# Three of four loads of an upsampling kernel issued from ScalarE's queue instead of SyncE's

## The chip, the cores and the metric

The kernel runs on one core of a Trainium2 chip. The metric is the device time in microseconds of one execution; the median of several runs is given. A profile of one execution shows what each engine and each DMA queue did, on a clock that starts with the core's first recorded instruction. Its length is called the span.

## The reference

Nearest-neighbour upsampling by 2 in both directions: every input value is written four times. The input is 16 x 64 x 64 x 64 in float32 (16.78 MB), the output 16 x 64 x 128 x 128 (67.11 MB).

```python
for i in range(new_h):
    for j in range(new_w):
        result[:, :, i, j] = x[:, :, i // scale_factor, j // scale_factor]
```

## The kernel before

The 65,536 image rows of 64 values are laid over 128 partitions, so each partition holds R = 512 rows, contiguous in DRAM. One SBUF tile, `mem`, holds everything: at its end the whole input (`xt`, 512 x 64 values for each partition), in front of that a free part of 79 rows' output size.

The input comes in four loads (line 195), all issued from SyncE: rows 0 to 8, 8 to 256, 256 to 480 and 480 to 512. They are called load 1 to load 4 here.

The output is made in nine steps (store 0 to store 8, with `rows = [52, 40, 52, 63, 52, 64, 63, 63, 63]` input rows for each partition). In each step VectorE expands 9/16 of the step's rows (line 215) and ScalarE the others (line 216) into a part of `mem`, and a DMA stores the result. Stores 2 to 6 are issued from GpSimd (line 218), the other four from SyncE (line 222). The steps' output places alternate between the start of `mem` and its end, where they overwrite input rows that have been read already; so a copy waits for the store that used its place before, and each engine waits for semaphores only. Nothing is planned by cost: the order on each queue is the order of the program.

The first store has one more wait, put in by hand: it is held until load 3 has landed ("stores begin as the loads end"). Both halves of step 0 need load 2, and VectorE's half needs load 1 too.

Two functions edit the built program at its end. `begin_before_barrier` takes SyncE's first four instructions, the loads, and puts them in front of SyncE's drain in the opening block, so that they are issued ahead of the barrier of all engines (line 249) that opens the kernel. `close_early` rearranges the closing barrier, so that only the last store is waited for at the end.

ScalarE has an activation table load behind the opening barrier, then its copies.

Of the kernel before, what the change touches and what calls it, by code (L numbers as in the profile page):

```python
# [6 lines left out]

EARLY = 4  # L10


def begin_before_barrier(nc):

    blocks = nc.main_func.blocks
    main, body = blocks[0], blocks[1]
    sp = mybir.EngineType.SP
    loads = [i for i in body.instructions if i.engine == sp][:EARLY]  # L20
    for load in loads:
        assert isinstance(load, mybir.InstDMACopy), type(load)
        assert not (load.sync_info and load.sync_info.on_wait)
    names = [i.name for i in loads]
    body.instructions = [i for i in body.instructions if i.name not in names]
    kept = list(main.instructions)
    at = next(
        n
        for n, i in enumerate(kept)
        if i.engine == sp and isinstance(i, mybir.InstDrain)  # L30
    )
    kept[at:at] = loads
    main.instructions = kept


def close_on_gpsimd(nc):
# [117 lines left out]
@with_exitstack  # L154
def kernel(
    ctx: ExitStack,
    tc: tile.TileContext,
    x: bass.AP,
    scale_factor: int,
    out: bass.AP,  # L160
):
    nc = tc.nc
    nc.at_finalize(begin_before_barrier)
    nc.at_finalize(close_early)
    P = nc.NUM_PARTITIONS
    s = int(scale_factor)
    B, C, H, W = x.shape
    R = B * C * H // P
    fdt = x.dtype

    xp = x.rearrange("b c h w -> (b c h) w").rearrange("(p r) w -> p r w", p=P)
    op = out.rearrange("b c (h hd) w -> (b c h) (hd w)", hd=s).rearrange(
        "(p r) w -> p r w", p=P
    )

    rows = [52, 40, 52, 63, 52, 64, 63, 63, 63]
    GROW = s * s
    FREE = 79
    WF = FREE * GROW * W
    assert sum(rows) == R
    mem_pool = ctx.enter_context(tc.tile_pool(name="mem", bufs=1))
    mem = mem_pool.tile([P, WF + R * W], fdt, name="mem")
    xt = mem[:, WF:].rearrange("p (r w) -> p r w", r=R)

    HEAD = 8
    cuts = [0, HEAD, R // 2, R - 32, R]
    loads = [
        nc.sync.dma_start(out=xt[:, lo:hi], in_=xp[:, lo:hi])  # L195
        for lo, hi in zip(cuts, cuts[1:])
    ]

    def expanded(r0, r1):
        return (  # L200
            xt[:, r0:r1].unsqueeze(2).unsqueeze(4).to_broadcast([P, r1 - r0, s, W, s])
        )

    r0 = 0
    before = (0, 0)
    for n, k in enumerate(rows):
        size = k * GROW * W
        at = 0 if n % 2 == 0 else WF + r0 * W - size
        assert at >= before[1] or at + size <= before[0]
        before = (at, at + size)  # L210
        u = mem[:, at : at + size].rearrange(
            "p (k a w b) -> p k a w b", k=k, a=s, w=W
        )
        kv = k * 9 // 16
        nc.vector.tensor_copy(out=u[:, :kv], in_=expanded(r0, r0 + kv))  # L215
        nc.scalar.copy(out=u[:, kv:], in_=expanded(r0 + kv, r0 + k))  # L216
        if 2 <= n < len(rows) - 2:
            store = nc.gpsimd.dma_start(  # L218
                out=op[:, r0 : r0 + k, :], in_=u, single_packet=True
            )  # L220
        else:
            store = nc.sync.dma_start(out=op[:, r0 : r0 + k, :], in_=u)  # L222
        if n == 0:
            tc.add_manual_dep(
                store.ins,
                loads[-2].ins.name,
                mybir.DependencyInfo(
                    mybir.DependencyClass.Sync, mybir.DependencyReason.DATA
                ),
                reason="stores begin as the loads end",  # L230
            )
        r0 += k
# [35 lines left out]
```

## Time and the profile before

| what | value |
|---|---|
| runs, median (lowest to highest) | 197.26 us (197.16 to 197.34) |
| profiled execution: span | 195.8 us |
| profiled execution: its own time | not listed apart from its span; the span is 1.5 us below the median of the runs |
| VectorE, ScalarE, GpSimd busy | 69.6, 51.4, 3.0 us |
| bytes moved, mean rate | 83.89 MB, 428 GB/s |
| load 2 issued from SyncE to landing | 21.3 us |
| load 3 issued from SyncE to landing | 37.8 us |

The profile calls the engines DVE (VectorE), ACT (ScalarE), POOL (GpSimd) and SP (SyncE); "SPq" and "ACTq" are the queues of instructions that are not counted as work, such as DMA issues, drains and waits. "L195" is line 195 of the kernel. In a row of tenths, each digit is the busy share of one of 40 equal slices. A chain lists, in order of time, start, length and what the time went to, followed back from the last instruction.

### The profile page before, as it was taken

To read this page: it belongs to the slowest core of one execution; us is meant where nothing else is said; L and a number is where in the kernel's file an instruction comes from. 1 tells how busy PE (TensorE), PEld (TensorE's weight loads), DVE (VectorE), ACT (ScalarE), POOL (GpSimd) and SP (SyncE) were. 2 spreads that over 40 slices of the span, in tenths; PEclk is the share of its full clock that TensorE was granted. 3 is DMA by queue.
4 is the path that set the end of the run, shared out by engine and by line. 5 is a ranking of instruction groups with operands and counts; after the bars stand their busy time and mean duration, and the time that the engine had idled before them with its cause. 6 is when DMAs were issued, how large, how long until landed. Compare 5 with 4: busy or idle time off the path is not lost.

```text
span 195.8 us, 108 instructions
## 1 busy us (share of the span) xinstructions
DVE 69.6 (36%) x9; ACT 51.4 (26%) x10; POOL 3.0 (2%) x9
## 2 busy tenths in 40 slices
DVE  0000596000039289069007205930692002960000
ACT  2000548000036083063920006666000003900000
POOL 0000000000000100100100100010000000000000
DMA  9999889699899989899999899999999999999994
GB/s 391 493 415 415 375 387 551 295 455 522 348 442 418 537 370 500 370 422 422 422 422 522 348 522 428 428 428 428 422 422 422 422 422 422 448 514 501 435 422 211
DMA packets 1872, 83.89 MB, mean 428 GB/s; under 512 B 208, under 2 KB 208, under 8 KB 336
## 3 DMA queue, kind: packets, MB, share of 16 engines
q1 hardware_dynamic: 1152, 45.35, 53.8%
q0 software_dynamic: 720, 38.54, 45.4%
HBM read 16.78 MB, written 67.11 MB: 428 GB/s over the span
## 4 chain that ended last, share of the span: by engine, by line
DMA 73%; DVE 15%; issue 1%; SPq 1%; DVEq 0%; POOLq 0%
DMA out_dram<-mem 54%; DMA mem<-in_x_dram 19%; DVE mem L215 15%; SPq L195 0%; SPq L222 0%; DVEq L215 0%; POOLq L218 0%; POOLq L263 0%
## 5 line engine op out<-in xcount | busy, mean ns | idle before, releaser
L215 DVE COPY mem<-mem 128x8960 f32<-128x8960 f32 (+3 forms) x9 | 69.6, 7739 | 104.9 <-DMA out_dram<-mem 83.1
L216 ACT COPY mem<-mem 128x7168 f32<-128x7168 f32 (+2 forms) x9 | 50.1, 5572 | 117.5 <-DMA out_dram<-mem 89.8
L218 POOL DMA_DIRECT2D out_dram<-mem x5 | 2.8, 560 | 126.8 <-DVE mem L215 111.2
L216 ACT ACT_TABLE_LOAD x1 | 1.3, 1283 | 2.2 <-PEq L249 2.2
L249 POOL MEMSET const-float32-0.0<- 128x1 f32 x1 | 0.1, 99 | 0.2 <-issue 0.2
L249 POOL MEMSET const-bfloat16-1.0<- 128x1 bf16 x1 | 0.1, 102 | 0.0
L249 POOL MEMSET const-float32-1.0<- 128x1 f32 x1 | 0.1, 99 | 0.0
L249 POOL MEMSET const-uint8-127<- 128x1 uint8 x1 | 0.1, 99 | 0.0
## 6 DMA issues: line engine op xcount, KB each, us to landing
out_dram<-mem POOLq DMA_DIRECT2D x2, 8064.0 KB, 29.9
out_dram<-mem SPq DMA_DIRECT2D x2, 8064.0 KB, 24.8
out_dram<-mem POOLq DMA_DIRECT2D x2, 6656.0 KB, 22.6
mem<-in_x_dram SPq DMA_DIRECT2D x1, 7936.0 KB, 21.3
mem<-in_x_dram SPq DMA_DIRECT2D x1, 7168.0 KB, 37.8
out_dram<-mem SPq DMA_DIRECT2D x1, 6656.0 KB, 18.1
out_dram<-mem SPq DMA_DIRECT2D x1, 5120.0 KB, 29.7
mem<-in_x_dram SPq DMA_DIRECT2D x1, 1024.0 KB, 39.8
```

The lines of the kernel that those rows point to most:

```text
L215: nc.vector.tensor_copy(out=u[:, :kv], in_=expanded(r0, r0 + kv))
L216: nc.scalar.copy(out=u[:, kv:], in_=expanded(r0 + kv, r0 + k))
L218: store = nc.gpsimd.dma_start(out=op[:, r0 : r0 + k, :], in_=u, single_packet=True)
L249: nc = _bacc.Bacc("TRN2", target_bir_lowering=False, num_devices=1)
```

## The change

Load 1 stays on SyncE's queue; loads 2, 3 and 4 are issued from ScalarE's. The function that moves loads ahead of the opening barrier now does so for both engines: one load in front of SyncE's drain, three in front of ScalarE's. Line numbers behind the edit grow by two. Nothing else differs: the copies, the stores, the hand-made wait and the places in `mem` are the same.

```diff
-EARLY = 4
+EARLY = {mybir.EngineType.SP: 1, mybir.EngineType.Activation: 3}
...
-    sp = mybir.EngineType.SP
-    loads = [i for i in body.instructions if i.engine == sp][:EARLY]
...
-    at = next(
-        n
-        for n, i in enumerate(kept)
-        if i.engine == sp and isinstance(i, mybir.InstDrain)
-    )
-    kept[at:at] = loads
-    main.instructions = kept
+    for engine, count in EARLY.items():
+        loads = [
+            i
+            for i in body.instructions
+            if i.engine == engine and isinstance(i, mybir.InstDMACopy)
+        ][:count]
...
+        at = next(
+            n
+            for n, i in enumerate(kept)
+            if i.engine == engine and isinstance(i, mybir.InstDrain)
+        )
+        kept[at:at] = loads
+        main.instructions = kept
...
     cuts = [0, HEAD, R // 2, R - 32, R]
+    queues = [nc.sync, nc.scalar, nc.scalar, nc.scalar]
     loads = [
-        nc.sync.dma_start(out=xt[:, lo:hi], in_=xp[:, lo:hi])
-        for lo, hi in zip(cuts, cuts[1:])
+        queue.dma_start(out=xt[:, lo:hi], in_=xp[:, lo:hi])
+        for queue, lo, hi in zip(queues, cuts, cuts[1:])
     ]
```

More of the change, by code (lines that the diff above doesn't have):

```diff
@@ L18, in begin_before_barrier @@
     main, body = blocks[0], blocks[1]
-    sp = mybir.EngineType.SP
-    loads = [i for i in body.instructions if i.engine == sp][:EARLY]
[L21 to L26, printed above, removed]
-    at = next(
-        n
-        for n, i in enumerate(kept)
-        if i.engine == sp and isinstance(i, mybir.InstDrain)
-    )
-    kept[at:at] = loads
-    main.instructions = kept
+    for engine, count in EARLY.items():
[4 more added lines that the diff above has]
+        ][:count]
+        assert len(loads) == count
+        assert not any(i.sync_info and i.sync_info.on_wait for i in loads)
+        names = [i.name for i in loads]
+        body.instructions = [i for i in body.instructions if i.name not in names]
+        kept = list(main.instructions)
+        at = next(
[5 more added lines that the diff above has]
+        main.instructions = kept
 def close_on_gpsimd(nc):
```

## The prediction

> **What bounds the kernel now.** I read the page first: busy time and queues, then the chain that ended last.
>
> ```profile
> span 195.8 us, 108 instructions
> ...
> DVE 69.6 (36%) x9; ACT 51.4 (26%) x10; POOL 3.0 (2%) x9
> ...
> DMA  9999889699899989899999899999999999999994
> ...
> q1 hardware_dynamic: 1152, 45.35, 53.8%
> q0 software_dynamic: 720, 38.54, 45.4%
> ...
> DMA 73%; DVE 15%; issue 1%; SPq 1%; DVEq 0%; POOLq 0%
> ```
>
> VectorE and ScalarE are idle two thirds of the time. The DMA queues' packets fill 53.8 + 45.4 = 99.2% of what 16 engines have in 195.8 us: the kernel is a transfer of 83.89 MB. The chain in order of time, merged, shows where it starts and where it is handed on:
>
> ```profile
> 0.00 0.37 SPq L195
> 0.37 0.05 issue
> 0.42 0.42 SPq L195
> 0.85 0.04 issue
> 0.89 37.79 DMA mem<-in_x_dram
> ...
> 38.77 0.35 SPq L222
> ...
> 39.29 29.69 DMA out_dram<-mem
> ...
> 79.15 40.20 DMA out_dram<-mem x2
> ...
> 129.52 35.38 DMA out_dram<-mem
> ```
>
> Rates by stage, from landings on this chain. The load of 1,024 KB and the first two stores (12,800 KB, 13.11 MB) land between 38.68 and 68.97: 433 GB/s. The next three stores (21.89 MB) land between there and 119.35: 434 GB/s. The last four (33.16 MB) run to 195.77: 434 GB/s. The first three loads, 15.73 MB, would take 36.2 us at 434, yet land at 38.68. So all slack is about 2.4 us at the very start, before the stream runs at full rate; later the engines never run dry. A change of queues can win only there, and can lose wherever it makes a gap.
>
> The start, from the packet records of the trace: load 1 (8 rows) is issued at 0.00, its first packet starts at 1.005 and the 16 engines finish it between 1.73 and 2.28. Load 2 (248 rows) is issued at 0.42. Its packets, 63,488 bytes each, take 2.342 us in the steady part; the engines begin their second one between 4.52 and 5.05, so the first counts as a full-rate packet started between 2.18 and 2.70. Between the end of load 1 and that point each engine loses 0.42 to 0.45 us on average: it has run out of load 1 and load 2 is not flowing yet. That is all this change can reach.
>
> **The change part by part.** *Load 2 moves to the front of another queue.* In SyncE's queue it stood behind one issue of 0.37 and a gap of 0.05, and began at 0.42. On ScalarE nothing stands in front of it. When ScalarE gets there is seen from the opening barrier, line 249 (minimum, median and maximum in ns, then first and last start in us), and what an issue costs from line 195:
>
> ```profile
> L249 ACTq DRAIN  x1: 8/8/8, 0.1 to 0.1; - x1
> ```
>
> ```profile
> L195 SPq DMA_DIRECT2D mem<-in_x_dram x4: 373/428/432, 0.0 to 1.4; - x4
> ```
>
> ScalarE's drain starts at 0.127 in the record, and the loads are put just ahead of it. So load 2 is issued at 0.13 instead of 0.42, 0.30 us earlier. No DMA is issued by ScalarE in the trace of before. I bound its cost by the nearest rows: 0.33 to 0.43 for SyncE's issues, 0.53 to 0.67 for GpSimd's. I take SyncE's 0.37 to 0.43, since these are the same transfers, byte for byte. At the upper end, 0.67, load 2's issue would end at 0.80, against 0.42 + 0.42 = 0.85 now, so even GpSimd's issue cost leaves 0.05. Below, a cheaper issue gains little more: load 2 cannot flow before load 1's packets are through, 0.42 to 0.45 earlier than now. The lead of 0.30 lies inside that cap, so I count it whole: **-0.30 us**, bounds 0 and -0.45.
>
> The Trainium skill speaks against hoping for more: "DMA: Bandwidth & Descriptors", section "Issuing engines are not separate DMA queues", says that DMAs from several engines run on the same 16 DMA engines and that issuing them concurrently saves only the sequencer's issue time. By that rule the sum would be at most one issue, -0.42 us and 196.84. The stages at 433 to 434 GB/s above, which mix SyncE's and GpSimd's stores, agree that another queue adds no rate.
>
> *Load 1 now shares the engines with load 2.* It was alone in front; now its 8 packets per engine alternate with load 2's. Store 6 (GpSimd) and store 7 (SyncE) show how two queues share: the DVE copy released by store 5 starts at 138.78, so store 6 had the engines from about 138.7. Alone it would need 19.0 us and land at 157.6; it landed at 164.90, 7.3 us or three of store 7's 2.38 us packets later, and no rate was lost. So load 1 may land near 20 us instead of 2.6. The only readers of its rows are the first VectorE copy, which waits for load 2 as well (21.77), and the second store at 39. Cost nothing; cover 0 to 2 us for the copy, and then 4.9 us more, because the copies end at 33.8 and the first store waits for load 3 until 38.68.
>
> *Loads 3 and 4* are issued from ScalarE at about 0.6 and 1.05, needed by the engines at 21 and 38. Load 4's tail no longer stands ahead of store 0 in one queue: store 0 (issued 38.77, descriptors about 1.0 later) alternates with what is left of load 4, which ends at 41.16 today. The same bytes, so store 0 and store 1 land as before; load 4 may land some 2 to 4 us later. Its only readers are the last copies, whose wait for it begins at 129 at the earliest. Nothing.
>
> *ScalarE's queue:* three issues, 0.13 + 3 x 0.43 + 2 x 0.05 = 1.5 us, now ahead of its drain; SyncE's drain, which ended the barrier at 1.85 + 0.13, comes at 0.4. ScalarE becomes the last to arrive, about 0.35 earlier, and the table load moves from 2.20 to about 1.85 (timeline):
>
> ```profile
> 2.20 1.28 ACT L216 ACT_TABLE_LOAD   x1 [2.20 <-PEq L249]
> ...
> 21.77 5.10 ACT L216 COPY mem<-mem 128x5888 f32<-128x5888 f32 x1 [18.29 <-DMA mem<-in_x_dram]
> ```
>
> It is followed by 18.3 us of waiting for load 2: cover enough. GpSimd's first store is at 65.5. SyncE has no work between 0.4 and 38.7. No wait is added behind which anything queues.
>
> *To the end.* Every later step hangs on a landing, and every landing on the one stream, so -0.30 travels through if each handover keeps its slack. The tightest: store 8 is issued at 174.55, needs about 1.0 until its first packet (load 1's row), and the engines end store 7 between 176.06 and 176.36: 0.5 us over. It hangs on store 6's landing, which moves with the rest.
>
> Sum: span 195.8 - 0.30 = 195.5. The page gives no other time for that execution; its span stands 1.47 below the median of the runs, 197.26 (197.16 to 197.34), for what lies around it. With that unchanged: **196.96 us**, -0.15%.
>
> **The rivals.**
>
> *A. No gain (about 197.26, 197.1 to 197.4).* The 0.42 between the loads is not load 2's issue but the delay of 16 engines starting long reads of DRAM together, or the two queues' descriptors are made one after the other. For it: first packets of load 2 on engines that began at once still took up to 2.86 to 3.08 instead of 2.34. Against: the engine that began last, at 2.57, took 2.38, as if the wait ends at a common time after the issue. Then load 2's second packets still begin at 4.5 to 5.05.
>
> *B. The whole issue is saved (196.84, 196.7 to 196.87).* ScalarE comes to its first load at 0.00 as SyncE does, and 0.42 goes. For: the cap of 0.42 to 0.45 allows it. Against: the drain at 0.127, with nothing listed before it.
>
> *C. ScalarE's issue is late (197.7 to 198.0).* Its first DMA needs longer from issue to first packet than SyncE's second one. It decides where that excess passes 0.30 us; each 0.1 beyond costs 0.1. With an excess of 0.7 to 1.0, as large as load 1's whole 1.0 delay, the time rises by 0.4 to 0.7. For: the trace has no DMA of ScalarE at all. Against: the same kind of issue on SyncE and its first packet at 1.005, without a prior one to warm it.
>
> *D. Alternation of small and large reads leaves gaps (198.0 to 200.3).* Each 2 KB packet lasts 84 ns, too short to cover the start of a large read on the other queue; 8 such gaps of 0.42 are 3.4 us, less the lead of 0.30; from the first gap on the lead is gone, and two or three make 198.0. For: the 0.42 occurred just where 2 KB packets gave way to large ones. Against: stores 6 and 7 alternated without loss, and a 4-byte semaphore packet between load 2 and load 3 cost no delay (the packets on either side at 2.342 and 2.116).
>
> That the change does not do what it says (loads left behind the barrier, issued after 2.1) I rule out: in the order of the built program the three loads stand before ScalarE's barrier wait.
>
> **How the numbers follow.** About 0.2%, 0.39 us, is what a measurement of this kernel can tell from no change; so "faster" needs a time under 196.87, "slower" one over 197.65. The forecast has 0.47, A 0.20, B 0.12, C 0.12, D 0.09. Faster: B and a part of 0.09 of the forecast that reaches the cap, 0.21. Slower: C and D, 0.21. Within: the rest, 0.58. The range 196.6 to 198.0 takes in the cap of 0.45 with 0.2 for the runs' own spread below, and C above; it leaves out most of D. The likeliest case alone is 196.8 to 197.1.
>
> **What would show it.** Right: ScalarE's first load at 0.1 with an issue of 0.37 to 0.43; load 2's second packets from 4.2 to 4.75; loads 2 and 3 landing near 21.4 and 38.4; load 1 landing late; every later landing 0.3 earlier; the end of the span at 195.5. Wrong: load 2 landing at 21.7 or later (A, C), packets of 2.34 separated by gaps while load 1 lasts (D), or a new gap between stores 0, 1 and 2 or ahead of store 8, whose engines today run on without one.

## The result: the changed kernel is 0.3% slower

The changed kernel takes 198.06 us (median of 22 runs, 197.14 to 198.43), the kernel before 197.23 beside it (22 runs, 197.03 to 199.95). The medians are 0.83 us apart; the ratio on record, which goes by all runs and not by the medians, is 1.003, interval 1.002 to 1.0041. The forecast was 196.96 with a range up to 198.0. The profiled execution took 198.16 with a span of 196.8, so 1.36 lies outside the span. In the other runs on record it is 1.3 to 1.4 for both kernels: the loss is inside the span.

The queue rows of the page and the merged chain of the kernel after, to be held against those of before; q10 is the new queue, ScalarE's:

```profile
span 196.8 us, 108 instructions
...
q0 software_dynamic: 720, 38.54, 45.4%
q1 hardware_dynamic: 720, 28.84, 34.2%
q10 hardware_dynamic: 432, 16.52, 19.4%
```

```profile
0.12 0.38 ACTq L197
...
0.52 38.59 DMA mem<-in_x_dram
...
39.71 29.69 DMA out_dram<-mem
...
79.58 40.48 DMA out_dram<-mem x2
...
130.23 35.53 DMA out_dram<-mem
```

The DMA engines are as full as before (99.0% of the span). The first DMA piece now ends at 39.11 instead of 38.68, the next at 69.40 instead of 68.97, then 120.06 instead of 119.35 and 165.76 instead of 164.90, and the span ends 1.05 later. So 0.43 is lost ahead of the first store and 0.62 more while stores 2 to 8 run. (These are two profiled executions, 1.05 apart; the medians are 0.83 apart.) The timeline of the first microseconds shows the change done as meant:

```profile
0.00 0.37 SPq L197 DMA_DIRECT2D mem<-in_x_dram  x1
0.12 1.34 ACTq L197 DMA_DIRECT2D mem<-in_x_dram  x3
...
1.87 1.28 ACT L218 ACT_TABLE_LOAD   x1 [1.87 <-PEq L251]
22.18 5.10 ACT L218 COPY mem<-mem 128x5888 f32<-128x5888 f32 x1 [19.03 <-DMA mem<-in_x_dram]
```

ScalarE issues load 2 at 0.12, and yet its copy starts at 22.18 instead of 21.77. The landing rows for load 2 and load 1, in us from issue, before and then after:

```profile
mem<-in_x_dram SPq DMA_DIRECT2D x1, 7936.0 KB, 21.3
...
mem<-in_x_dram SPq DMA_DIRECT2D x1, 256.0 KB, 2.6
```

```profile
mem<-in_x_dram ACTq DMA_DIRECT2D x1, 7936.0 KB, 22.0
...
mem<-in_x_dram SPq DMA_DIRECT2D x1, 256.0 KB, 3.5
```

Load 1 takes 3.5 instead of 2.6. The packet records (one for each piece that a DMA engine moves) show where: its 2 KB packets, of which the longest took 0.59, now take up to 0.91, and the last ends at 3.12 instead of 2.28. The 16 DMA engines begin load 2's second packet between 4.46 and 5.46, on average 4.95 (before: 4.52 to 5.04, average 4.77). A load has landed when the slowest engine is done, and that one is 0.42 later: 0.18 is the later mean, the rest the wider spread.

The loss in the stores is read from the packet records too. Packets of one size mostly take the same time: 1.966 us for 53,248 bytes, 1.514 for 40,960, 2.380 for 64,512, 2.418 for 65,536. What a packet took beyond that is called its loss here, and added up over the packets of an engine. The records do not name the engine; it is found by joining a packet's end to the next one's start, so that sums over all engines are firm, and figures of one engine an estimate (counts of engines are good to one or two). An engine that loses over 0.03 us in store 0 is called disturbed. In the kernel before, no engine lost anything in stores 0 to 2, and the mean over the 16 engines for stores 0 to 5 together is 0.03 us. After, 12 engines are disturbed, and the means are 0.06, 0.05, 0.11, 0.07, 0.07 and 0.09 in stores 0 to 5, in all 0.46.

The 0.46 has two parts. About 0.25 is in single packets that are over 0.02 us too long, mostly by 0.02 to 0.1; most of them start some 0.1 to 3 us after the issue of the next store. About 0.20 is in many packets that are longer by 0.002 to 0.02 us: 75 of the 128 packets of store 0, where the kernel before has none.

### The profile page after: what moved, and what is told of

It is laid out like the page before. It is cut to its first block, busy times and chain, and to the rows that moved or that the text cites. A ratio compares the mean times of both kernels' runs of the same rounds, so it can differ in the third digit from the quotient of the medians.

```text
span 196.8 us, 108 instructions
## 1 busy us (share of the span) xinstructions
DVE 69.6 (35%) x9; ACT 51.4 (26%) x10; POOL 3.0 (2%) x9
## 4 chain that ended last, share of the span: by engine, by line
DMA 73%; DVE 14%; issue 1%; SPq 0%; ACTq 0%; DVEq 0%; POOLq 0%
DMA out_dram<-mem 54%; DMA mem<-in_x_dram 20%; DVE mem L217 14%; SPq L224 0%; ACTq L197 0%; DVEq L217 0%; POOLq L220 0%; POOLq L265 0%
```

## The experiments

All but two of them change the loads only. One table holds what was measured: when load 2 lands, how many DMA engines are disturbed, the mean loss of an engine in stores 0 to 5, the span (all four from the one profiled run), the median of all runs, and the ratio to the kernel before beside it.

| kernel | load 2 lands | engines | loss | span | median | ratio (interval) |
|---|---|---|---|---|---|---|
| before | 21.74 | 0 | 0.03 | 195.8 | 197.23 | |
| after | 22.16 | 12 | 0.46 | 196.8 | 198.06 | 1.003 (1.002 to 1.0041) |
| all_act | 21.91 | 1 | 0.10 | 196.5 | 197.28 | 0.9997 (0.9979 to 1.0016) |
| load1_act | 22.05 | 9 | 0.36 | 196.7 | 197.97 | 1.0028 (1.0014 to 1.0043) |
| load4_late_act | 21.62 | 1 | 0.16 | 196.3 | 197.75 | 1.0021 (1.0006 to 1.0037) |
| load4_late_sp | 22.28 | 16 | 0.60 | 197.1 | 198.33 | 1.0048 (1.0033 to 1.0064) |
| act_behind | 24.25 | 13 | 0.53 | 198.3 | 199.01 | 1.007 (1.0046 to 1.0094) |
| head13_sp | 21.72 | 2 | 0.14 | 196.5 | 197.71 | 0.9998 (0.9977 to 1.002) |
| head24_sp | 21.87 | 7 | 0.27 | 196.5 | 197.75 | 1.0015 (1.0 to 1.0031) |
| merged_sp | 21.89 | 3 | 0.21 | 196.4 | 197.18 | 0.9999 (0.9982 to 1.0016) |
| one_row_act | 21.70 | 2 | 0.12 | 196.2 | 197.51 | 1.0007 (0.9992 to 1.0021) |
| head1_after | 21.89 | 1 | 0.06 | 196.3 | 197.22 | 1.0001 (0.9989 to 1.0013) |
| sp_stores_before | 21.74 | 0 | 0.00 | 195.7 | 197.13 | 0.9999 (0.9987 to 1.001) |
| sp_stores_after | 21.98 | 8 | 0.18 | 196.3 | 197.63 | 1.0019 (1.0007 to 1.0032) |
| row_first | 22.04 | 1 | 0.13 | 196.5 | 197.57 | 1.0019 (1.0002 to 1.0035) |
| head4_after | 21.79 | 1 | 0.08 | 196.3 | 197.67 | 1.0015 (1.0001 to 1.0029) |
| head24_after | 21.99 | 11 | 0.46 | 196.6 | 198.17 | 1.0047 (1.0035 to 1.0059) |

How the columns hang together: the end is set by the slowest engine, so one disturbed engine is enough. In the profiled run of all_act (197.81) one engine lost 0.69 in stores 0 to 5, the next less than 0.3, and that one was last; 10 of its 12 runs lie between 197.14 and 197.45. The same holds for head13_sp (0.69), row_first (0.66) and load4_late_act (0.5 to 0.7): the engine that loses most is the last at the end of store 5. The kernels with one or two disturbed engines have runs near 197.1 and others mostly at 197.5 to 197.9, so their medians say little. Only one run of each was profiled, so that the faster runs lack the disturbed engine is likely and not shown, and load4_late_act, with no run under 197.6, does not fit. Kernels with eight or more disturbed engines have hardly a run under 197.5 (after: 2 of 22; load1_act, load4_late_sp, act_behind, sp_stores_after and head24_after: none of 46; the kernel before: 15 of 22 to 29 of 35).

### Is it ScalarE's queue, the start, or the handover to store 0?

all_act puts all four loads on ScalarE; load1_act puts load 1 there and leaves the others on SyncE; load4_late_act is the kernel before with load 4 issued from ScalarE behind the second copy; load4_late_sp is the changed kernel with load 4 on SyncE there. (EARLY, the count of loads in front of the barrier, goes with the queues in each.)

```diff
# all_act
-queues = [nc.sync, nc.scalar, nc.scalar, nc.scalar]
+queues = [nc.scalar, nc.scalar, nc.scalar, nc.scalar]
# load1_act
+queues = [nc.scalar, nc.sync, nc.sync, nc.sync]
# load4_late_act (load4_late_sp: nc.sync, with loads 2 and 3 on ScalarE)
+queues = [nc.sync, nc.sync, nc.sync]
...
+        if n == 1:
+            last = nc.scalar.dma_start(out=xt[:, cuts[3] :], in_=xp[:, cuts[3] :])
+            tc.add_manual_dep(last.ins, copy.ins.name, ...)
```

(In load4_late_act the second store waits for load 3 too.)

> All four loads on ScalarE's queue, one behind the other; nothing competes at the start, but a load queue other than the stores' is in use. Theory 1 (start): with load 1 and load 2 on two queues the 16 engines' first reads compete, load 1's packets end as late as 3.1 us and the slowest engine begins load 2's second packet at 5.46 instead of 5.05. Then here the start is as in the kernel before, later only by ScalarE's 0.12: second packets 4.6 to 5.2, load 2 lands near 21.9. Theory 2 (handover): store 0 on another queue than load 4 makes the engines lose 0.05 to 0.15 us at each later store. Then the losses in the stores (0.6 us up to the end) stay here: span near 196.4. Rival: both come from the competition at the start: span near 195.9. Rival: ScalarE's queue itself is slower: load 2 lands at 22.2 or later.

> Mirror of the change: load 1 alone on ScalarE's queue, loads 2 to 4 on SyncE's, in front of the barrier. Theory 1: the same competition at the start, spread of the second packets about 1 us (before 0.53), load 2 lands at 22.0 to 22.2. Theory 2 (load 4 and store 0 on one queue again): no losses in the stores, span 196.2. Rival, competition or a spread start causes the losses too: span 196.6 to 196.9. Rival, ScalarE's queue slow for large loads: load 2 lands at 21.4 to 21.7, span 195.5 to 195.8.

> The kernel before, with load 4 alone issued from ScalarE, behind the second copy (about 34 us). The start is that of the kernel before (load 2 lands near 21.74). Theory 2, the handover from load 4 to store 0 across two queues: the stores lose about 0.6 us, span 196.4. Rival, the losses come from the start: span 195.7 to 195.9.

> The changed kernel, with load 4 back on SyncE's queue, issued there behind VectorE's second copy (about 33 us), so that store 0 stands behind it in the same queue. The start is that of the changed kernel (load 2 lands near 22.16). Theory 2: no losses in the stores, span about 196.2, and at most 0.3 more where load 4 alternates with load 3. Rival, the losses come from the start: span 196.8.

all_act: load 2 at 21.91, one engine disturbed, median 197.28. ScalarE's queue is not slow; load 2 lands 0.17 later, and the first issue is 0.12 later. (The span of its profiled run, 196.5, is near what theory 2 expected; of its other 11 runs, 10 have spans of 195.8 to 196.1.) Theory 2, the handover from load 4 to store 0, falls as the cause of the change's loss: load4_late_sp has the handover in one queue and is no better than the change (16 engines, 198.33), and all_act, like head1_after below, has it across two queues and is no slower than the kernel before (0.9997 and 1.0001). load4_late_act came out as theory 2 expected, though: a span of 196.3, and every run at 197.6 or above, with one disturbed engine. Load 4 issued late from another queue costs something of its own there; why is open. load1_act points to the start again, but not as theory 1 had it: the landing row of load 1 is

```profile
mem<-in_x_dram ACTq DMA_DIRECT2D x1, 256.0 KB, 21.9
```

Here load 2 was first on every engine, and load 1's eight packets went one by one between load 2's. The spread of the second packets is only 0.54, so engines can be disturbed without a wide spread; load 2 shares the engines with load 1 up to the end, and lands at 22.05. This alternation is what the Trainium skill says in "DMA: Bandwidth & Descriptors", section "Queues, rings and completion order": an engine goes round between the queue rows that have work, packet by packet. The trace agrees, with 256 KB that take 21.9 us. (In the changed kernel all of load 1's packets came before load 2's first on each engine, and nothing alternated.)

### Is there a gap to fill at the start, and does it take two queues?

act_behind is the changed kernel with ScalarE's loads behind the barrier. The others are the kernel before, all on SyncE, with another size of load 1: 13 rows, 24 rows, or loads 1 and 2 in one.

```diff
# act_behind
-EARLY = {mybir.EngineType.SP: 1, mybir.EngineType.Activation: 3}
+EARLY = {mybir.EngineType.SP: 1}
# head13_sp, head24_sp
-    HEAD = 8
+    HEAD = 13   # 24
# merged_sp (EARLY = 3)
-    cuts = [0, HEAD, R // 2, R - 32, R]
+    cuts = [0, R // 2, R - 32, R]
```

> The changed kernel with ScalarE's three loads behind the opening barrier: load 2 is issued near 0.85 us, when load 1's descriptors are already out, so the two loads' reads hardly meet, but the queues are those of the changed kernel. Theory 3 (what makes the engines lose time at every store is that reads of two queues overlapped at the start): no such losses, 16 engines start load 2 within about 0.6 us, load 2 lands near 22.15 (0.42 late by its issue alone), span 196.2. Rival, the second load queue makes the losses: span 196.8 with 10 or more engines losing 0.05 us or more in store 0.

> The kernel before, all on SyncE, with 13 rows in load 1 instead of 8: its packets last some 0.38 us longer for each engine, about the 0.42 to 0.45 that the engines lack work between load 1 and load 2. If that gap is there to be filled: load 2 lands 0.3 to 0.4 earlier (21.35 to 21.45), span 195.4. Rival, the gap is a delay behind load 1 whatever its length: load 2 lands as before, 21.74. Theory 4 (losses come where load 2's first packet follows load 1 with its read already done, on whatever queue): some engines lose 0.05 or more in store 0 and the span is 195.6 to 196.1; theory 3: none lose, 195.4.

> The kernel before, all on SyncE, with 24 rows in load 1: load 2's descriptors are there well before load 1 ends, so its first packet takes 2.2 to 2.3 us with its read hidden, in one queue. Load 2 lands 0.4 earlier (21.3). Theory 4: most engines lose 0.05 or more in store 0, span 195.9 to 196.2. Theory 3 (two queues have to overlap): no losses, span 195.3 to 195.5.

> The kernel before, with loads 1 and 2 as one load of 256 rows on SyncE, issued at 0.00: nothing before it, nothing beside it. Its first packets start at 1.0 and wait for their reads (3 us instead of 2.42), since no small load fills that time; load 2 lands 0.1 to 0.3 later than in the kernel before (21.85 to 22.05). Theories 3 and 4: no losses in the stores, span 195.9 to 196.1. If the start spread or the earlier issue were what makes losses: span 196.6.

The gap of 0.42 between load 1 and load 2 that the prediction wanted to use gave nothing when it was filled or avoided. With 13 rows in load 1, load 2's first packets take 2.29 to 2.33 us, nearly as the later ones (2.295), so there is no gap any more, and load 2 lands at 21.72, as before. merged_sp issues its load at 0.00 and lands at 21.89; its chain:

```profile
0.00 0.38 SPq L195
...
0.43 38.41 DMA mem<-in_x_dram
```

Rows up to 480 are in at 38.84 instead of 38.68. However the first 8 MB (rows 0 to 256) were cut on one queue, and whether load 2's rows were issued at 0.00 or 0.42, they were in at 21.6 to 21.9. An estimate says the same: take the first packet at 1.005, count each engine's packets of load 1 and its first one of load 2 at their usual times, and compare with the mean start of the second packet. The engines are then 0.76 us behind in the kernel before, 0.82 in merged_sp, 0.69 in head13_sp and 0.80 in head24_sp, and 0.93 in the changed kernel. So about 0.7 to 0.8 us is lost at the start with any load 1, or none; what the engines wait for there is not shown.

head24_sp has 7 disturbed engines on one queue: theory 3, that it takes two queues, is too strong. Theory 4 fares no better: load 2's first packets run at their usual time on every engine in head13_sp and head24_sp, with 2 and 7 disturbed engines, and merged_sp, which has no load 1, has 3. act_behind speaks against theory 3 from the other side:

```profile
0.78 0.37 ACTq L197
...
1.18 40.02 DMA mem<-in_x_dram
```

Load 2 goes out at 0.78; its first packet starts at 1.82, and load 1's last one ends at 2.35. Three engines begin load 2 only at 3.4 to 4.0, it lands at 24.25, 13 engines are disturbed, and the kernel is the slowest of all. Why is not known.

### Two queues at work, load 1's bytes, and GpSimd's stores

```diff
# one_row_act: the kernel before, the last row alone on ScalarE
+    cuts = [0, HEAD, R // 2, R - 32, R - 1, R]
+    queues = [nc.sync, nc.sync, nc.sync, nc.sync, nc.scalar]
# head1_after: the changed kernel
-    HEAD = 8
+    HEAD = 1
# sp_stores_before, sp_stores_after
-        if 2 <= n < len(rows) - 2:
+        if False:
```

> The kernel before, with one row (the last) cut off load 4 and issued from ScalarE in front of the barrier; loads 1 and 2 stay together on SyncE. Theory 5 (two queues at work at the start are enough to bring most engines into the state that loses at every store): 9 or more engines lose over 0.03 us in store 0, runs at 197.7 or above. Theory 6 (it takes load 1 and load 2 on different queues): at most 3 engines lose in store 0, mean loss over stores 0 to 5 under 0.25 us, most runs near 197.2.

> The changed kernel with one row in load 1 instead of 8, so SyncE's queue carries 32 KB in packets of 256 bytes beside load 2. If load 1's reads, slowed by load 2's, spread the engines, the spread of the engines shrinks: load 2 lands near 21.8 instead of 22.16. Theory 6: still 9 or more engines lose in store 0, span 196.3 to 196.5. Rival, the loss needs the volume of load 1: under 4 engines lose, span 195.9.

> The kernel before with stores 2 to 6 issued from SyncE too. Theory 7: the time that engines lose in stores 2 to 5 goes with GpSimd's issue of the next store (0.1 us each), since stores 7 and 8 from SyncE cost 0.02; then every run is near 197.1 or below, without those at 197.6 to 198.4. Rival, the loss comes at each new store whatever its queue: the runs spread as now, 197.0 to 198.4.

> The changed kernel with stores 2 to 6 issued from SyncE too. Load 2 still lands near 22.16 (start spread 1 us). Theory 7: the loss in stores 2 to 6 goes, 0.4 us of the 0.6; span 196.2 to 196.4. Rival: the engines lose as before at each store, span 196.8.

one_row_act has two queues at work at the start and 2 disturbed engines: theory 5 falls, though 9 of its 12 runs lie at 197.48 to 197.62 and not near 197.2. head1_after is the change itself with one row in load 1: load 2 lands at 21.89, one engine is disturbed, 197.22. So theory 6, two queues for loads 1 and 2, falls too: it takes load 1's bytes.

sp_stores_after has the changed kernel's start (load 2 at 21.98, last second packet at 5.25), but from store 1's landing, 69.18, to the end it takes 127.09 us, where the changed kernel takes 127.39 and the kernel before 126.78. Its median is 0.43 under the changed kernel's, though not beside it. So of the 0.61 that the change loses there, 0.30 goes when GpSimd issues no store. The packets show which part: the mean loss in stores 0 to 5 falls from 0.46 to 0.18, and most of what goes is in the single long packets (0.25 to 0.04), while the many slightly longer ones stay (0.20 to 0.14). Two things limit this. Store 0, which runs ahead of any GpSimd issue, has 8 disturbed engines here and 12 in the changed kernel, so part of the difference is the start of this one run. And the stores now stand in one queue, so whether GpSimd's issue or a second queue makes the long packets is not separated. In sp_stores_before not one packet of stores 0 to 5 is longer than usual. Its median is no different (197.13 against 197.15), and theory 7 expected every run near 197.1 or below, but four lie at 197.3 to 197.5 and one at 197.77.

### Load 2's lead, or the queue?

row_first leaves all queues as in the change and takes away the lead: ScalarE issues one row first, and so load 2 at 0.52. Two more vary load 1 in the changed kernel.

```diff
# row_first
+    parts = [
+        (nc.sync, 0, HEAD),
+        (nc.scalar, R - 1, R),
+        (nc.scalar, HEAD, R // 2),
+        (nc.scalar, R // 2, R - 32),
+        (nc.scalar, R - 32, R - 1),
+    ]
# head4_after, head24_after
-    HEAD = 8
+    HEAD = 4   # 24
```

> The changed kernel, with the last row cut off load 4 and issued from ScalarE ahead of load 2, which so goes out near 0.53 us instead of 0.12; queues otherwise as in the changed kernel. If the harm is load 2's lead (its long reads meet load 1's short ones): load 1's packets end near 2.4, the 16 engines' spread is 0.6 or less, load 2 lands at 21.8 to 21.95, fewer than 4 engines lose in store 0, span 196.0. If it is the two loads being on different queues: load 2 lands at 22.1 or later, 9 or more engines lose, span 196.7.

> The changed kernel with 4 rows in load 1, half the bytes that meet load 2's reads. If the harm grows with load 1's bytes (8 rows: load 2 at 22.16 and 12 engines losing in store 0; 1 row: 21.89 and 1 engine): load 2 lands near 22.0, 3 to 9 engines lose, runs near 197.6. If any load 1 beyond a row's size does the whole harm: as with 8 rows, 198.0.

> The changed kernel with 24 rows in load 1, three times the bytes that meet load 2's reads. If the harm grows with load 1's bytes: load 2 lands later than 22.16, most engines lose in store 0, runs at 198.1 or above. Rival, longer packets in load 1 keep the engines together (one queue with 24 rows: spread 0.49, 197.75): load 2 lands near 21.9, runs near 197.7.

```profile
mem<-in_x_dram SPq DMA_DIRECT2D x1, 256.0 KB, 2.7
```

```profile
0.52 0.45 ACTq L203
...
1.00 37.97 DMA mem<-in_x_dram
```

In row_first, with the same two queues, load 1 is in after 2.7 as it was on one queue (its packets end at 2.29, the longest takes 0.56), and one engine is disturbed instead of 12. So most of the disturbance goes with the 0.41 by which load 2 is issued earlier in the changed kernel, and the separate queue alone does not bring it in this run. It does not all go: load 2 lands at 22.04, where 21.8 to 21.95 was expected (0.1 of it by the issue, which is 0.1 later than in the kernel before), half of the runs are under 197.5 and the others at 197.8 or above, and the ratio is still 1.0019. The added row also puts small packets of its own between the two loads; that was not tested apart.

With 4 rows load 2 lands at 21.79 and one engine is disturbed, not the 3 to 9 expected; with 24 rows, 11 engines, load 2 at 21.99 and no run under 197.9. For 1, 4, 8 and 24 rows the ratios to the kernel before are 1.0001, 1.0015, 1.003 and 1.0047 and the medians 197.22, 197.67, 198.06 and 198.17: the time grows with load 1's bytes. The disturbed engines of the one profiled run each, 1, 1, 12 and 11, look like a step instead, and load 2's landing, 21.89, 21.79, 22.16 and 21.99, does not grow with the bytes at all. With 24 rows a part of load 1 does alternate with load 2: its last packet ends at 12.83, and it lands at 15.41.

How far one profile can be trusted on the start: four kernels have the start of the kernel before (before, load4_late_act, one_row_act, sp_stores_before) and land load 2 at 21.62 to 21.74; three have the changed one (after, load4_late_sp, sp_stores_after) and land it at 21.98 to 22.28. The two groups don't touch, and neither do the mean starts of the second packet (4.68 to 4.77 and 4.88 to 5.17). The spread of the second packets is less sure: 0.43 to 0.70 in the first group, 0.70 to 1.00 in the second.

## Why the prediction was wrong

- *ScalarE's issues*: right. Predicted at 0.13 with 0.37 to 0.43 us; measured 0.12, with 0.375 for load 2 and 0.45 for the next two. Rival C, a late issue, is out by this and by all_act, where the first packet starts 1.0 after ScalarE's issue, as after SyncE's. That its 197.7 to 198.0 lies close to the result is chance.
- *The term of -0.30 us* is the step that failed, in sign: +0.42. It rested on reading the 0.42 to 0.45 between load 1 and load 2 as waiting for load 2's issue. merged_sp (0.42 earlier, no gain) and head13_sp (gap filled, no gain) show that this reading was wrong, as rival A had it; the rival was given 0.20. That the delay comes of the engines starting long reads together, which was A's reason, is not shown apart. What A lacked is that the lead itself does harm: load 1's packets slow down, the engines begin load 2's second packet 0.18 later on average and over 1.0 us instead of 0.52, and the slowest one counts. I had looked at the range of the engines only to find a cap for the gain.
- *"Travels through if each handover keeps its slack"* failed too. The handovers are not what was lost; the packets themselves became longer. The 434 GB/s of the stores was taken for a fixed rate; with 12 disturbed engines it was 432 from store 1's landing to the end. This is the larger term, 0.62 of the 1.05 between the two profiled runs.
- *Load 1 alternates with load 2 and costs nothing*: not in this kernel, where its packets came first and it landed at 3.46; where it did alternate (load1_act) the kernel was slower (1.0028). (The place of its rows is overwritten already by ScalarE's second copy, at 29.81 before, and not first used by the second store at 39; with load 1 in at 3.46 that changed nothing.)
- *Loads 3 and 4, the handover to store 0*: no harm from where they stand in the change, by all_act and head1_after; load 4 landed 0.43 later with the rest, not 2 to 4. *ScalarE's queue and the table load*: 1.87 against a predicted 1.85, covered by 19.03 us.
- *Rival D* named a time near the result (198.0 to 200.3) by another mechanism, gaps between alternating packets. Nothing alternated, so this too is chance.
- *The runs' own spread* was read off three runs, 197.16 to 197.34. Of the 22 beside the result 7 lie above 197.5, up to 199.95, and the range allowed 0.2 for it.
- *The rule of the Trainium skill* ("DMA: Bandwidth & Descriptors", "Issuing engines are not separate DMA queues"), that another queue saves only issue time, held as an upper bound: load 2's issue came 0.31 us earlier, and nothing more was saved: the median is 0.83 higher.

What stays open: what it is in an engine that, once disturbed, makes it lose time at nearly every later store. It goes with load 2 being issued close behind a load 1 of 8 or more rows in after, load4_late_sp, head24_after and, on one queue, head24_sp; but the kernel before has load 1 of 8 rows and load 2 at 0.42 on one queue and no disturbed engine. In load1_act load 1's packets came in among load 2's; act_behind and load4_late_act do not fit. The single long packets mostly go when no store comes from GpSimd; the many slightly longer ones stay without a name.

None of these kernels is measurably faster than the kernel before; the lowest ratio, that of all_act, is 0.9997 (0.9979 to 1.0016), and the lowest median, that of sp_stores_before, 197.13.

## What to carry to other kernels

Idle time between two transfers at the start of a stream is not proof that the second one waits for its issue: put other bytes into it, or issue earlier, before counting it as gain. Where a transfer is spread over 16 engines, follow the slowest engine: an edit that moves the mean a little (0.18 here) can move the end more (0.42) by spreading the engines. In this kernel no order was better than the small first load followed by the large one in the same queue; issued beside it from another queue the large one landed later, and issued there 0.78 behind it (act_behind) it was later still.

## What the runs showed that I had not expected

- An engine that has begun to lose time at stores mostly goes on: 0.05 to 0.15 us for each, up to nearly 0.8 in stores 0 to 5 (load4_late_sp), while in other kernels some lose nothing in the same run (all_act). The profiled runs with one such engine took 197.61 to 197.83, where the kernel before has most runs near 197.1.
- Small packets take longer with large ones issued 0.12 us behind them on another queue: 2 KB packets at the start took up to 0.91 us instead of 0.59 (up to 1.08 in load4_late_sp). With the large ones at 0.52 it was 0.56 (row_first).
- The first 8 MB are in at 21.6 to 21.9 whether load 1 has no rows of its own, 8, 13 or 24, on one queue.
